# Where a norm's weight is multiplied in: into the weight units, or into the tokens' hi/lo parts (with the residual read from memory)

## The chip, the cores and the metric

The kernel runs on one core of a Trainium2 chip. The metric is the device time of one execution in microseconds, as the median over several runs. The core has five engines that run side by side, each with its own instruction queue: TensorE (PE, matmuls; PEld is its weight load), VectorE (DVE), ScalarE (ACT), GpSimd (POOL) and SyncE (SP), which in this kernel only issues DMAs. POOL issues some DMAs as well. An engine works its queue strictly in order, and a DMA-issuing instruction waits in its queue like any other. Instructions on different engines wait for each other by semaphores.

## The reference: what is computed

One inference step of a decoder trunk with two layers over T = 1032 tokens (1024 of a prompt, 8 decode tokens) and 1024 model dimensions, all in fp32. The parts that matter here:

```python
def rms_norm(x, w):
    y = x32 * lax.rsqrt(jnp.mean(x32 * x32, axis=-1, keepdims=True) + NORM_EPS)
    return (y * w.astype(jnp.float32)).astype(x.dtype)

for layer in range(DEPTH):                       # DEPTH = 2
    h = rms_norm(x, norm_mix[layer])
    if layer % 2 == 0:                           # layer 0: gated delta rule + retention
        out, ... = hybrid_mixer(h, ...)          # input projection, mixers, output projection w_out
    else:                                        # layer 1: state-space mixer
        out, ... = ssd_mixer(h, ...)
    x = x + out
    x = x + squared_relu_mlp(rms_norm(x, norm_mlp[layer]), mlp_w1[layer], mlp_w2[layer])
return rms_norm(x, norm_final), ...
```

Every sub-layer thus begins with a projection of `x * rstd * w`: `rstd` is one number for each token, `w` one number for each model dimension. The projection sums over the model dimension, so `w` can be multiplied into the rows of the weight matrix or into the rows of `x`, while `rstd` can be multiplied in after the sum.

## The kernel before

Tokens are kept transposed: 8 row tiles of 128 model dimensions by 1032 tokens. A product is made of three matmuls in a reduced format of fp32 (fp32r): each operand is split into a hi part and a lo part, and `mm3` (L147) adds whi·xhi (L150), whi·xlo (L151) and wlo·xhi (L152). The tokens' parts are the tiles `xh[k]` and `xl[k]`, which stay in SBUF for the length of a sub-layer; token columns go in three pieces of 344 (`NSL`).

**Weights.** `load_w` (L132) brings a unit of up to 512 columns from memory into `raw` (3 buffers, DMA from SP's queue, L136). If a norm weight is given, POOL multiplies the unit by it, in place (L140). ACT then rounds it to `whi` (L144), and DVE, or POOL for the units of the output and down projections, subtracts to get `wlo` (L145). `whi` and `wlo` share 6 buffers. The 264 units of the input projections (`wih`, `wis`) and of the MLP's up projections (`w` at `w1`) pass through L140; the units of the output projections (`woh`, `wos`) and of the down projections (`w2`) don't.

**Tokens.** At the start, `load_x` (L296) loads the 8 tiles of x (`xr`), and for each ACT rounds it to `xh` (L345) and DVE subtracts to `xl` (L346); POOL, ACT and DVE square and sum for the norm (L327, L328, L332). Later splits are made piece by piece by `split_piece` (L225), right after the last addition to a residual piece: ACT copies to `xh` (L229), DVE subtracts to `xl` (L230), ACT squares, POOL adds the square (L241). `rsqrt` (L243, its instruction is L250) is a POOL instruction everywhere, for the norms inside the mixers too (`rry`, `rs`, `nrs`).

**Stages in time.** Layer 0's mixer runs from 0 to about 735 us of the profiled execution, its last blocks of output projection to 800, its MLP to about 1520; layer 1's mixer runs to about 2320 and its MLP to the end. In a mixer, `proj` or `conv_tile`/`z` tiles are projected (72 units L140 fall between 1550 and 2250) while the recurrences of the chunks run in between: chains of small matmuls and DVE, ACT and POOL instructions. In layer 1's, POOL also multiplies the decode states (`dpr`, L1749, reduced by DVE at L1750) and issues the stores of states (L1747) and spilled outputs (L1505).

**Output projection.** Its weights are cut in blocks by input rows. The first block is done while the mixer's last work is running: `out_first` (L466) computes 8 row tiles m by 3 pieces n; DVE adds PSUM and `xh` into a stage tile `ost` (L473), POOL adds `xl` (L474), and SP stores it to `accd` in memory (L475). In layer 0 the pieces n = 0, 1 stage in a pair of buffers and n = 2 in a single one, so each is used once for each m; in layer 1 five buffers of two pools alternate. `out_proj` (L1328) then reloads the 8 sums (`acc<-accd`, L1335) and adds the later blocks into them (L1342); the last block's pieces are split at once by `split_piece`. `xh` and `xl` of the layer's input thus serve both as matmul operand and as the residual.

**MLP.** `up` projects a hidden tile, applies relu and the square (L1225 to L1228), and after each 4 tiles `down` (L1231) adds their part to `acc` (L1236). The last `down` of layer 0 splits its sums for layer 1; the last layer ends with `finish` (L1241), which takes the final norm in.

**Order.** The code is recorded once and scheduled by the framework, which puts each engine's instructions in the order of its own simulated times; the buffers' reuse makes the waits. The diff's places in the program therefore don't say where an instruction ends up in its queue.

Of the kernel before, what the change touches and what calls it, by code (L numbers as in the profile page):

```python
# [14 lines left out]
ALU = mybir.AluOpType  # L15
# [80 lines left out]
class Kern:  # L96
    def __init__(self, ctx, tc, I, O):
# [20 lines left out]
        self.xl = [self.xp.tile([P, T], F32R, name=f"xl{k}") for k in range(KT)]  # L118

# [12 lines left out]
    def load_w(self, src, n, normw=None, lo_eng=None, dst=None, norm_eng=None):  # L132
# [4 lines left out]
        if normw is not None:  # L137
            k = normw.shape[1]
            r3 = raw[:, :n].rearrange("p (k c) -> p k c", k=k)
            (norm_eng or nc.gpsimd).tensor_tensor(out=r3, in0=r3, in1=normw.unsqueeze(2).to_broadcast([P, k, n // k]), op=ALU.mult)  # L140
# [13 lines left out]
    def load_half(self, src, kh, M, normw):  # L154
        return self.load_w(src[:, kh * 4 * M:(kh + 1) * 4 * M], 4 * M, normw[:, kh * 4:kh * 4 + 4])
# [9 lines left out]
    def products(self, src, M, normw, pss):  # L165

        for kh in range(2):
            hi, lo = self.ahead.pop(0) if self.ahead else self.load_half(src, kh, M, normw)
# [12 lines left out]
    def gemm_units(self, src, M, normw, evict, other=False):  # L181
# [11 lines left out]
        for u, n in enumerate(self.products(src, M, normw, pss)):  # L193
# [13 lines left out]
    def gemm_flush(self, src, parts, evict):  # L207
# [3 lines left out]
        for m in range(8):  # L211
            w = []
            for k0 in range(0, kn, cut):
                k1 = min(kn, k0 + cut)
                hi, lo = self.load_w(src(m)[:, k0 * 128:k1 * 128], (k1 - k0) * 128, None, self.nc.gpsimd)
                w += [(hi[:, i:i + 128], lo[:, i:i + 128]) for i in range(0, (k1 - k0) * 128, 128)]
# [79 lines left out]
    def load_x(self, gp):  # L296
# [16 lines left out]
        w0 = [self.load_half(I["wih"][0], 0, 128, normw)]  # L313
# [30 lines left out]
        for m in range(KT):  # L344
            nc.scalar.copy(self.xh[m], xr[m])  # L345
            nc.vector.tensor_tensor(out=self.xl[m], in0=xr[m], in1=self.xh[m].bitcast(F32), op=ALU.subtract)  # L346
# [4 lines left out]
            if m == 1:  # L351
                w0.append(self.load_half(I["wih"][0], 1, 128, normw))
# [1552 lines left out]
```

## Time and profile before

| | |
|---|---|
| time, median of 3 runs | 3217.74 us (3217.33 to 3217.88) |
| profiled execution | 3203.04 us |
| its span (first to last instruction) | 3200.8 us |
| mean clock granted to TensorE | 0.973 |
| busy: PE / DVE / ACT / POOL | 3052.8 / 1724.0 / 841.2 / 1264.1 us |
| L140 on POOL | 264 instructions, 306.2 us |
| L474 on POOL | 48 instructions, median 928 ns |

The profiled execution is 14.7 us shorter than the median of the timed runs; 2.2 us of its time lie outside its span. A row of the profile names a line of the code, the engine, the operation, and the tiles by `out<-in`. In rows of a group, `x264 | 306.2, 1161 | 636.8 <-DMA raw<-w 330.0` means 264 instructions, 306.2 us busy, 1161 ns each, and 636.8 us in which the engine idled just before them, 330.0 of it until that DMA ended. In rows of the timeline the first number is the start in us, the second the duration, and brackets give the idle time just before it and what ended it. A row of a window gives, for each engine, its busy time in that stretch and, after PEclk, the granted clock.

### The profile page before, as it was taken

The numbers are of one execution on the slowest core, as the hardware profiler recorded it, in microseconds if no ns is written. First come the engines' busy times: TensorE is split into PE (matmuls) and PEld (weight loads), VectorE is DVE, ScalarE is ACT, GpSimd is POOL, SyncE is SP. The second block draws the span as 40 slices with busy tenths as digits, with TensorE's granted clock in tenths as the row PEclk, the third lists the DMA queues.
The fourth block names the chain that finished last, engine by engine and source line by source line (L and its number), as shares of the span: only waits on it lengthen the run. The fifth ranks groups of instructions, "written<-read, shape, count | busy, mean of one in ns | idle before, by whom it ended". The sixth has DMA issues, their size and how long they took to land. (4 is left out here: it accounts for less than half of the span.)

```text
span 3200.8 us, 49506 instructions
## 1 busy us (share of the span) xinstructions
PE 3052.8 (95%) x19758; PEld 2918.4 (91%) x19758; DVE 1724.0 (54%) x3189; ACT 841.2 (26%) x1604; POOL 1264.1 (39%) x1234
## 2 busy tenths in 40 slices
PE   7999999989999999999998999999899999999998
PEld 6888888879999999999987988897899999999998
DVE  7664767464333333335888696978635333333334
ACT  3221222214111111114344434343214111111112
POOL 4332324146323323335246556556625233232224
PEclk8899999889999999999999999999999999999999
DMA  3011103133111111111112121222531111111112
GB/s 122 23 44 59 47 22 105 42 132 116 47 47 47 47 48 48 48 47 46 42 52 65 50 84 58 80 74 96 186 109 44 50 47 47 47 47 47 47 49 71
DMA packets 102326, 202.14 MB, mean 63 GB/s; under 512 B 12624, under 2 KB 27728, under 8 KB 102096
## 3 DMA queue, kind: packets, MB, share of 16 engines
q1 hardware_dynamic: 94800, 173.82, 17.4%
q0 software_dynamic: 7296, 25.17, 2.0%
q8 instruction: 155, 2.54, 0.3%
q14 instruction: 75, 0.61, 0.1%
HBM read 157.94 MB, written 38.89 MB: 61 GB/s over the span
## 5 line engine op out<-in xcount | busy, mean ns | idle before, releaser
L150 PE MATMUL pg<-xh,whi 128*128 128x344 f32 x3072 | 1003.2, 327 | 10.8 <-DVE sxc L1460 4.8
L151 PE MATMUL pg<-xl,whi 128*128 128x344 f32 x3072 | 998.2, 325 | 0.0
L152 PE MATMUL pg<-xh,wlo 128*128 128x344 f32 x3072 | 997.2, 325 | 0.7 <-DVE wlo L145 0.7
L150 PEld LDWEIGHTS pg<-xh,whi 128*128 128x128 f32 x3072 | 585.5, 191 | 18.4 <-DVE sxc L1460 5.8
L144 ACT CAST whi<-raw 128x512 fp32r<-128x512 f32 (+2 forms) x443 | 271.6, 613 | 1257.9 <-PE pg L151 859.2
L152 PEld LDWEIGHTS pg<-xh,wlo 128*128 128x128 f32 x3072 | 585.2, 191 | 4.5 <-issue 1.7
L151 PEld LDWEIGHTS pg<-xl,whi 128*128 128x128 f32 x3072 | 584.2, 190 | 4.8 <-issue 2.8
L140 POOL TENSOR_TENSOR raw<-raw,vec 128x512 f32<-128x512 f32 x264 | 306.2, 1161 | 636.8 <-DMA raw<-w 330.0
L151 PE MATMUL pg<-alo,whi 128*128 128x344 f32 (+2 forms) x1476 | 472.4, 320 | 0.0
L152 PE MATMUL pg<-ahi,wlo 128*128 128x344 f32 (+2 forms) x1476 | 472.3, 320 | 0.0
L150 PE MATMUL pg<-ahi,whi 128*128 128x344 f32 (+2 forms) x1476 | 471.5, 319 | 0.0
L1236 DVE TENSOR_TENSOR acc<-acc,pg 128x344 f32<-128x344 f32 x360 | 183.1, 512 | 385.0 <-PE pg L152 384.7
L145 POOL TENSOR_TENSOR wlo<-raw,whi 128x512 fp32r<-128x512 f32 (+2 forms) x179 | 225.2, 1260 | 328.4 <-ACT whi L144 327.4
L145 DVE TENSOR_TENSOR wlo<-raw,whi 128x512 fp32r<-128x512 f32 x264 | 198.4, 752 | 195.6 <-ACT whi L144 185.8
L1227 POOL TENSOR_TENSOR r<-r 128x344 f32<-128x344 f32 x192 | 146.1, 762 | 386.0 <-ACT ahi L1226 337.3
L152 PEld LDWEIGHTS pg<-ahi,wlo 128*128 128x128 f32 x1476 | 277.6, 188 | 0.0
L150 PEld LDWEIGHTS pg<-ahi,whi 128*128 128x128 f32 x1476 | 277.5, 188 | 0.0
L151 PEld LDWEIGHTS pg<-alo,whi 128*128 128x128 f32 x1476 | 277.3, 188 | 0.0
L1228 DVE TENSOR_TENSOR alo<-r,ahi 128x344 fp32r<-128x344 f32 x192 | 135.5, 707 | 254.1 <-POOL r L1227 254.1
L1226 ACT ACTIVATE ahi<-r 128x344 fp32r<-128x344 f32 x192 | 94.7, 493 | 338.8 <-DVE r L1225 338.8
L1225 DVE SCALAR_TENSOR_TENSOR r<-pg,rstd_bc 128x344 f32<-128x344 f32 x186 | 94.9, 510 | 76.7 <-PE pg L152 75.4
L150 PE MATMUL pg<-mhi,whi 128*128 128x344 f32 x408 | 131.5, 323 | 4.9 <-DVE acc L1342 4.9
(540 smaller groups left out, 4439.8 us busy)
## 6 DMA issues: line engine op xcount, KB each, us to landing
raw<-w SPq DMA_DIRECT2D x256, 256.0 KB, 2.6
raw<-wis SPq DMA_DIRECT2D x80, 256.0 KB, 2.7
raw<-wih SPq DMA_DIRECT2D x56, 256.0 KB, 2.9
mraw<-spill SPq DMA_DIRECT2D x17, 512.0 KB, 4.1
accd<-ost SPq DMA_DIRECT2D x48, 172.0 KB, 2.5
acc<-accd SPq DMA_DIRECT2D x16, 516.0 KB, 6.9
dS<-sstate SPq DMA_DIRECT2D x32, 256.0 KB, 2.7
o_sssm<-dS POOLq DMA_DIRECT2D x32, 256.0 KB, 2.3
```

The costliest lines, as they stand in the source:

```text
L140: (norm_eng or nc.gpsimd).tensor_tensor(out=r3, in0=r3, in1=normw.unsqueeze(2).to_broadcast([P, k, n // k]), op=ALU.mult)
L144: nc.scalar.copy(hi[:, :n], raw[:, :n])
L145: (lo_eng or nc.vector).tensor_tensor(out=lo[:, :n], in0=raw[:, :n], in1=hi[:, :n].bitcast(F32), op=ALU.subtract)
L150: t.matmul(ps, lhsT=whi, rhs=xhi, start=start, stop=False)
L151: t.matmul(ps, lhsT=whi, rhs=xlo, start=False, stop=False)
L152: t.matmul(ps, lhsT=wlo, rhs=xhi, start=False, stop=stop)
L1225: nc.vector.scalar_tensor_tensor(out=r, in0=ps, scalar=0.0, in1=self.rstd_bc[:, s], op0=ALU.max, op1=ALU.mult)
L1226: nc.scalar.activation(hi[:, s], r, AF.Square)
L1227: nc.gpsimd.tensor_tensor(out=r, in0=r, in1=r, op=ALU.mult)
L1228: nc.vector.tensor_tensor(out=lo[:, s], in0=r, in1=hi[:, s].bitcast(F32), op=ALU.subtract)
L1236: nc.vector.tensor_tensor(out=s, in0=s, in1=ps, op=ALU.add)
```

## The change

The multiplication by the norm weight leaves `load_w` and goes into the split of the tokens: `xh` becomes the rounded `w*x`, and `xl` the rest of it, both with one scalar for each partition. ACT's copy becomes an activation with a scale (L229, L345), and DVE's subtraction an instruction that multiplies and subtracts (L230, L346). The 264 instructions at L140 and two small ones in the set-up of layer 1 (L1366) are gone.

`xh` and `xl` then no longer hold the residual. `out_first` now loads it from memory into the stage tile: in layer 0 from the kernel's input `xT`, in layer 1 from a new buffer `resd` in memory, which the last `down` of layer 0 fills, one DMA from POOL's queue for each m. DVE adds PSUM into the stage tile, and the addition on POOL (L474) is gone.

```diff
-    def load_w(self, src, n, normw=None, lo_eng=None, dst=None, norm_eng=None):
+    def load_w(self, src, n, lo_eng=None, dst=None):
...
         raw = self.wp.tile([P, 512], F32, tag="raw", name="raw", bufs=3)
         nc.sync.dma_start(raw[:, :n], src)
-        if normw is not None:
-            k = normw.shape[1]
-            r3 = raw[:, :n].rearrange("p (k c) -> p k c", k=k)
-            (norm_eng or nc.gpsimd).tensor_tensor(out=r3, in0=r3, in1=normw.unsqueeze(2).to_broadcast([P, k, n // k]), op=ALU.mult)
...
-    def split_piece(self, m, n, src, ssq, tp):
+    def split(self, m, s, src, w):
 
         nc = self.nc
-        s = NSL[n]
-        nc.scalar.copy(self.xh[m][:, s], src)
-        nc.vector.tensor_tensor(out=self.xl[m][:, s], in0=src, in1=self.xh[m][:, s].bitcast(F32), op=ALU.subtract)
+        nc.scalar.activation(self.xh[m][:, s], src, AF.Copy, scale=w)
+        nc.vector.scalar_tensor_tensor(out=self.xl[m][:, s], in0=src, scalar=w, in1=self.xh[m][:, s].bitcast(F32), op0=ALU.mult, op1=ALU.subtract)
+
+    def split_piece(self, m, n, src, ssq, tp, norm):
+
+        self.split(m, NSL[n], src, self.V(norm, m))
         self.square_piece(m, n, src, ssq, tp)
...
         for m in range(KT):
-            nc.scalar.copy(self.xh[m], xr[m])
-            nc.vector.tensor_tensor(out=self.xl[m], in0=xr[m], in1=self.xh[m].bitcast(F32), op=ALU.subtract)
+            self.split(m, slice(0, T), xr[m], self.V("mix0", m))
...
+            if l == 0:
+                self.resid = lambda m: self.I["xT"][:, m, :]
+            else:
+                self.resid = lambda m: self.resd[m]
...
             r = stage(n)
-            nc.vector.tensor_tensor(out=r, in0=ps, in1=self.xh[m][:, s].bitcast(F32), op=ALU.add)
-            nc.gpsimd.tensor_tensor(out=r, in0=r, in1=self.xl[m][:, s].bitcast(F32), op=ALU.add)
+            nc.sync.dma_start(r, self.resid(m)[:, s])
+            nc.vector.tensor_tensor(out=r, in0=r, in1=ps, op=ALU.add)
             nc.sync.dma_start(self.accd[m][:, s], r)
...
                     if b == HID // 4 - 1:
-                        self.split_piece(m, n, s, ssq, tp)
+                        self.split_piece(m, n, s, ssq, tp, "mix1")
+                        if n == 2:
+                            nc.gpsimd.dma_start(self.resd[m], acc[m])
...
-                nc.gpsimd.tensor_tensor(out=raw, in0=raw, in1=normw[:, k:k + 4].unsqueeze(2).to_broadcast([P, 4, 32]), op=ALU.mult)
```

What the schedule makes of it is seen in three places. The first is POOL's queue near the start of layer 1's chunks, at 1667 us of the profiled execution. Before:

```order
L1462 TENSOR_SCALAR sco<-sxc 128x11
L140 TENSOR_TENSOR raw<-raw,vec 128x512
L1749 TENSOR_TENSOR dpr<-dS,dbc 128x512 x2
L140 TENSOR_TENSOR raw<-raw,vec 128x512
L1457 MEMSET sxc 128x3
L1675 TENSOR_TENSOR x<-x,yi 128x4x128
L1682 TENSOR_TENSOR S<-S,segend 128x512
```

and with the change (lines are one lower there):

```order
L1461 TENSOR_SCALAR sco<-sxc 128x11
L1748 TENSOR_TENSOR dpr<-dS,dbc 128x512 x2
L1456 MEMSET sxc 128x3
L1674 TENSOR_TENSOR x<-x,yi 128x4x128
L1681 TENSOR_TENSOR S<-S,segend 128x512
```

The multiplications of weight units that stood ahead of and behind the two `dpr` are gone, and the rest keeps its order.

The second is SP's queue at the end of layer 0's `out_first`, at about 715 to 727 us, where the stores of the stage tiles, the loads of weight units and the reloads of the sums follow each other. Before:

```order
L475 DMA accd_6_103<-ost 128x344
L460 DMA mraw<-spill_7_96 128x1024
L136 DMA raw<-woh 128x384
L475 DMA accd_6_103<-ost 128x344
L475 DMA accd_7_104<-ost 128x344 x2
L136 DMA raw<-woh 128x256
L475 DMA accd_7_104<-ost 128x344
L1335 DMA acc_0_6973<-accd_0_97 128x1032
```

and with the change, where L477 is the load of the residual and L479 the store of the sum:

```order
L479 DMA accd_7_114<-ost 128x344
L477 DMA ost<-xT 128x344
L479 DMA accd_7_114<-ost 128x344
L138 DMA raw<-woh 128x256
L479 DMA accd_6_113<-ost 128x344
L477 DMA ost<-xT 128x344
L479 DMA accd_7_114<-ost 128x344
L138 DMA raw<-woh 128x384
L1338 DMA acc_0_6927<-accd_0_107 128x1032
```

The last piece of m = 7 now needs its load between the last store of m = 6 (the same stage buffer) and its own store, and all three stand ahead of the reloads of the sums in the one queue.

The third is POOL's queue at the border of the layers, about 1515 to 1540 us. Before:

```order
L241 TENSOR_TENSOR rstd_bc<-rstd_bc,sq 128x344 x2
L1393 MEMSET sx 128x288
L1457 MEMSET sxc 128x3 x2
L140 TENSOR_TENSOR raw<-raw,vec 128x512
L250 TENSOR_TENSOR rs<-ms,c_67 128x9
L140 TENSOR_TENSOR raw<-raw,vec 128x512 x2
L1462 TENSOR_SCALAR sco<-sxc 128x11
```

and with the change:

```order
L1241 DMA resd_95<-acc_6_6933 128x1032
L242 TENSOR_TENSOR rstd_bc<-rstd_bc,sq 128x344 x3
L1241 DMA resd_96<-acc_7_6934 128x1032
L242 TENSOR_TENSOR rstd_bc<-rstd_bc,sq 128x344
L1394 MEMSET sx 128x288
L251 TENSOR_TENSOR rs<-ms,c_67 128x9
L1456 MEMSET sxc 128x3 x2
L1461 TENSOR_SCALAR sco<-sxc 128x11
```

The stores of `resd` stand between the additions of squares, and the reciprocal root `rs` of the new norm has moved ahead of the two clears of `sxc`, with no weight unit in front of it.

More of the change, by code (lines that the diff above doesn't have):

```diff
@@ L118, in __init__ @@
         self.xl = [self.xp.tile([P, T], F32R, name=f"xl{k}") for k in range(KT)]
+        rp = ctx.enter_context(tc.tile_pool(name="resd", bufs=1, space=bass.MemoryType.DRAM))
+        self.resd = [rp.tile([P, T], F32, name=f"resd_{m}") for m in range(KT)]
     def V(self, name, i=0, n=1):
@@ L152, in mm3, with load_half @@
         t.matmul(ps, lhsT=wlo, rhs=xhi, start=False, stop=stop)
-    def load_half(self, src, kh, M, normw):
-        return self.load_w(src[:, kh * 4 * M:(kh + 1) * 4 * M], 4 * M, normw[:, kh * 4:kh * 4 + 4])
+    def load_half(self, src, kh, M):
+        return self.load_w(src[:, kh * 4 * M:(kh + 1) * 4 * M], 4 * M)
     def narrow(self, ps, w, x, k):
@@ L163, in narrow, with products @@
             self.nc.tensor.matmul(ps[32 * n:32 * n + M, 0:c.stop - c.start], lhsT=w, rhs=x[:, c], start=k == 0, stop=k == KT - 1)
-    def products(self, src, M, normw, pss):
+    def products(self, src, M, pss):
         for kh in range(2):
-            hi, lo = self.ahead.pop(0) if self.ahead else self.load_half(src, kh, M, normw)
+            hi, lo = self.ahead.pop(0) if self.ahead else self.load_half(src, kh, M)
             for n in range(3):
@@ L179, in others, with gemm_units @@
         return [self.pm(), self.ps2(), self.ps2()]
-    def gemm_units(self, src, M, normw, evict, other=False):
+    def gemm_units(self, src, M, evict, other=False):
         if self.first:
@@ L192, in gemm_units @@
         pss = self.others() if other else [self.pg() for n in range(3)]
-        for u, n in enumerate(self.products(src, M, normw, pss)):
+        for u, n in enumerate(self.products(src, M, pss)):
             if u == 0:
@@ L312, in load_x @@
         fetch(1)
-        w0 = [self.load_half(I["wih"][0], 0, 128, normw)]
+        w0 = [self.load_half(I["wih"][0], 0, 128)]
         nc.vector.tensor_scalar(out=self.ones_r, in0=self.ident, scalar1=0.0, scalar2=1.0, op0=ALU.mult, op1=ALU.add)
@@ L351, in load_x @@
             if m == 1:
-                w0.append(self.load_half(I["wih"][0], 1, 128, normw))
+                w0.append(self.load_half(I["wih"][0], 1, 128))
             if m > 1:
@@ L445, in layer @@
                 acc = [ap.tile([P, T], F32, name=f"acc{l}_{m}") for m in range(KT)]
-                self.out_proj(name, blocks, acc, tp, parts)
+                self.out_proj(name, blocks, acc, tp, parts, "mlp%d" % l)
             self.mlp(l, acc, l == 1)
@@ L486, in proj @@
         def proj(dst, off=0):
-            normw = self.V("mix0", 0, 8)
             def ev(n, ps):
                 nc.vector.tensor_tensor(out=dst[:, off + n * NW:off + (n + 1) * NW], in0=ps, in1=self.rstd_bc[:, NSL[n]], op=ALU.mult)
-            yield from self.gemm_units(I["wih"][next(wi)], 128, normw, ev)
+            yield from self.gemm_units(I["wih"][next(wi)], 128, ev)
         def gate(k, zs):
@@ L1228, in ev @@
                     nc.vector.tensor_tensor(out=lo[:, s], in0=r, in1=hi[:, s].bitcast(F32), op=ALU.subtract)
-                self.gemm_tile(I["w1"][l, t], 128, normw, ev, t == 1)
+                self.gemm_tile(I["w1"][l, t], 128, ev, t == 1)
             def down(b):
@@ L1325, in mlp, with out_proj @@
                 self.rstd = self.rstd_from()
-    def out_proj(self, name, blocks, acc, tp, parts):
+    def out_proj(self, name, blocks, acc, tp, parts, norm):
         nc, tc = self.nc, self.tc
@@ L1343, in ev @@
                     if last:
-                        self.split_piece(m, n, o, ssq, tp)
+                        self.split_piece(m, n, o, ssq, tp, norm)
                 for _ in self.gemm_flush(lambda m: self.I[name][m, :, c0 * 128:c0 * 128 + w], cur, ev):
@@ L1380, in ssm_setup @@
         self.first = self.others()
-        for u, _ in enumerate(self.products(I["wis"][4], 128, normw, self.first)):
+        for u, _ in enumerate(self.products(I["wis"][4], 128, self.first)):
             if u == 1:
@@ L1460, in ev @@
                 nc.vector.tensor_tensor(out=xc[:, 3 + n * NW:3 + (n + 1) * NW], in0=ps, in1=self.rstd_bc[:, NSL[n]], op=ALU.mult)
-            self.gemm_tile(I["wis"][ti // 4 * 10 + ti % 4 if ti < 16 else ti % 4 * 10 + ti // 4], 128, normw, ev)
+            self.gemm_tile(I["wis"][ti // 4 * 10 + ti % 4 if ti < 16 else ti % 4 * 10 + ti // 4], 128, ev)
             nc.gpsimd.tensor_scalar(out=gco, in0=xc[:, 3 + 1021:3 + 1032], scalar1=1.0, scalar2=None, op0=ALU.mult)
@@ L1485, in ev @@
                 nc.vector.scalar_tensor_tensor(out=z[:, NSL[n]], in0=ps, scalar=0.5, in1=self.rstd_bc[:, NSL[n]], op0=ALU.mult, op1=ALU.mult)
-            self.gemm_tile(I["wis"][g * 10 + 6 + i], 128, normw, ev)
+            self.gemm_tile(I["wis"][g * 10 + 6 + i], 128, ev)
             self.silu2(z, 1.0, gp)
```

7 lines of the change are left out of this document (2 added, 5 removed).

## The prediction

> **What bounds the kernel now.** First the page's head, then a table of windows cut at the stages (busy us and count for PE, PEld, DVE, ACT, POOL; then the granted clock, DMA share and GB/s).
>
> ```profile
> span 3200.8 us, 49506 instructions
> PE 3052.8 (95%) x19758; PEld 2918.4 (91%) x19758; DVE 1724.0 (54%) x3189; ACT 841.2 (26%) x1604; POOL 1264.1 (39%) x1234
> ...
> 0.00:40.00 40.00, 27.22 (x135) 17.02 (x135) 28.75 (x23) 17.08 (x21) 22.28 (x21) 0.87 0.58 187
> 40.00:640.00 600.00, 556.20 (x3838) 506.74 (x3836) 379.37 (x914) 150.06 (x316) 182.24 (x225) 0.92 0.16 49
> 640.00:735.00 95.00, 81.49 (x449) 69.93 (x449) 56.56 (x117) 20.17 (x36) 45.62 (x46) 0.87 0.45 153
> 735.00:800.00 65.00, 62.07 (x396) 61.01 (x395) 33.94 (x60) 27.30 (x62) 40.78 (x42) 1.00 0.24 82
> 800.00:1480.00 680.00, 680.00 (x4324) 680.00 (x4323) 238.97 (x427) 124.50 (x222) 209.87 (x214) 1.00 0.16 47
> 1480.00:1550.00 70.00, 67.43 (x436) 64.34 (x434) 50.48 (x93) 28.84 (x65) 39.46 (x41) 1.00 0.13 40
> 1550.00:2250.00 700.00, 652.03 (x4324) 598.40 (x4323) 559.95 (x884) 280.62 (x537) 385.61 (x320) 0.98 0.21 70
> 2250.00:2325.00 75.00, 64.99 (x397) 62.21 (x396) 42.01 (x72) 12.71 (x18) 44.13 (x41) 0.98 0.56 199
> ```
>
> TensorE sets the end: 148 us of the span (3200.8 - 3052.8) are all that any change outside it can win, short of a better clock. In the first MLP, 800 to 1480, PE idles 0.0 us, so nothing taken from POOL there is worth anything. The idle time lies in the mixers: 12.8 us at the start, 43.8 in 40 to 640, 13.5 in 640 to 735, 2.9 to 800, 2.6 at the layers' border, 48.0 in 1550 to 2250, 10.0 to 2325. There DVE is the busiest helper (559.95 of 700, 80%) and POOL is at 55%, so the question is how often POOL or DVE holds PE, and how often L140 or L474 is why.
>
> **What goes away, and where it lay.** The groups by line, the same windows for L140 alone, and the group of L474:
>
> ```profile
> L140 POOL TENSOR_TENSOR raw<-raw,vec 128x512 f32<-128x512 f32 x264 | 306.2, 1161 | 636.8 <-DMA raw<-w 330.0
> ...
> 40.00:640.00 600.00, 60.67 (x52) 0.92 0.16 49
> 1550.00:2250.00 700.00, 93.37 (x72) 0.98 0.21 70
> ...
> L474 POOL TENSOR_TENSOR ost<-ost,xl x48: 907/928/1916, 664.3 to 2310.4; 128x344 f32<-128x344 f32 x48
> ```
>
> Of 306.2 us only 154 lie in the two mixers, and they are not on PE's path as such: L140 acts by (a) standing in POOL's queue, often waiting for its DMA, ahead of an instruction that a chain needs, and (b) blocking DVE. I follow both through the timeline.
>
> **Layer 1's mixer, 1550 to 2250.** The clearest stall:
>
> ```profile
> 1704.39 1.04 POOL L140 TENSOR_TENSOR raw<-raw,vec 128x512 f32<-128x512 f32 x1 [0.49 <-DMA raw<-wis]
> 1705.39 2.62 POOL L1749 TENSOR_TENSOR dpr<-dS,dbc 128x512 f32<-128x512 f32 x2
> 1706.70 0.69 DVE L1750 TENSOR_REDUCE dy<-dpr 128x4 f32<-128x512 f32 x1 [2.31 <-POOL dpr L1749]
> ...
> 1709.38 0.48 PE L1665 MATMUL ps<-E,xdt 128*64 128x128 f32 x2 [2.85 <-DVE yi L1674]
> ...
> 1676.43 0.44 PE L1665 MATMUL ps<-E,xdt 128*64 128x128 f32 x4 [3.04 <-DVE yi L1674]
> 1805.59 0.33 PE L1665 MATMUL ps<-E,xdt 128*64 128x128 f32 x2 [1.15 <-DVE yi L1674]
> 2164.28 0.33 PE L1665 MATMUL ps<-E,xdt 128*64 128x128 f32 x2 [1.13 <-DVE yi L1674]
> 2051.14 1.19 PE L1677 MATMUL ps<-xd,sb 128*128 128x512 f32 x1 [2.19 <-DVE x L1667]
> ```
>
> L140 takes POOL at 1704.39 after 0.49 us of DMA wait; `dpr` starts 1.0 later for it, DVE waits 2.31 for `dpr`, and everything DVE has behind it, `yi` too, is late for PE. Without L140, `dpr` starts up to 1.5 us earlier (1.04 + 0.49), and DVE's wait shrinks by as much. Five stalls of PE have this chain (of the three small ones the first and the last stand above): 3.04 + 2.85 + 1.15 + 1.13 + 1.13 = 9.3 us; I take 6.4, since 1.5 of each of the first two come back and the three small ones can close (3.4). About a dozen more, of 0.5 to 2.2 us (the longest is the last row), follow a DVE instruction that was stretched while an L140 ran. They sum to about 15 us; I take a good third, 5.6, because DVE is 80% busy and its next instruction closes up only in part. Sum -12; from -5 (the five alone, halved) to -22 (nearly all of 24).
>
> On how DVE is stretched, the row at the kernel's start shows it plainly:
>
> ```profile
> 8.76 1.04 POOL L140 TENSOR_TENSOR raw<-raw,vec 128x512 f32<-128x512 f32 x1 [2.28 <-DMA raw<-wih]
> 8.85 2.04 DVE L346 TENSOR_TENSOR xl<-xr,xh 128x1032 fp32r<-128x1032 f32 x1 [0.78 <-ACT xh L345]
> ...
> 12.82 2.69 POOL L332 TENSOR_TENSOR sqx<-xr 128x1032 f32<-128x1032 f32 x1 [0.17 <-DMA xr<-xT]
> 13.67 2.39 DVE L145 TENSOR_TENSOR wlo<-raw,whi 128x512 fp32r<-128x512 f32 x1
> ...
> 16.11 0.46 PE L152 MATMUL pm<-xh,wlo 128*128 128x344 f32 x1 [3.16 <-DVE wlo L145]
> ```
>
> L145 takes 2.39 us beside POOL's L332 (12.82 to 15.51) against 0.68 alone, and L346 2.04 beside L140. [...]
>
> **The start, 0 to 40.** Without L140 at 8.76, L346 at 8.85 ends about 0.8 sooner (1.2 is its undisturbed time at 6.86), `whi` starts 1.08 earlier, and L145 falls before L332 rather than beside it. PE's 3.16 stall goes and some of what follows, while the first split must now wait for the norm weights: -5, from -8 to 0.
>
> **Layer 0's mixer, 40 to 800.** L140 stands ahead of `rry`, an rsqrt in the chain of the delta rule:
>
> ```profile
> 465.17 1.04 POOL L140 TENSOR_TENSOR raw<-raw,vec 128x512 f32<-128x512 f32 x1 [2.49 <-DMA raw<-wih]
> 466.16 1.04 POOL L250 TENSOR_TENSOR rry<-ssy,c 128x4 f32<-128x4 f32 x1
> 467.23 0.69 DVE L902 TENSOR_TENSOR Y<-Y,rry 128x512 f32<-128x512 f32 x1 [2.82 <-POOL rry L250]
> ...
> 467.98 0.33 PE L906 MATMUL ps<-c,Y 128*128 128x128 f32 x1 [2.50 <-DVE Y L902]
> ...
> 778.24 0.42 PE L152 MATMUL pg<-mhi,wlo 128*128 128x344 f32 x1 [1.81 <-POOL wlo L145]
> ```
>
> Two stalls of this kind (2.50 here, 1.43 at 169.93) and about 4 us of smaller ones after stretched DVE work: 40 to 640 gets -6, from -2 to -12 (a quarter of its 43.8). The 1.81 at 778.24 has an L140 1.5 us long ahead of the waited-for POOL work: -2, from -3 to 0.
>
> **Layer 0's `out_first`, the place that can lose.** Before, a stage buffer is used again once its store has landed; now it has to be stored, landed, loaded, landed and added into, and SP's one queue holds the load until the store has landed and everything behind it, the weight units of `woh` too.
>
> ```profile
> accd<-ost SPq DMA_DIRECT2D x48, 172.0 KB, 2.5
> raw<-woh SPq DMA_DIRECT2D x16, 192.0 KB, 2.5
> ...
> 710.37 0.52 DVE L473 TENSOR_TENSOR ost<-pg,xh 128x344 f32<-128x344 f32 x1 [2.37 <-DMA accd<-ost]
> 724.13 0.52 DVE L473 TENSOR_TENSOR ost<-pg,xh 128x344 f32<-128x344 f32 x1 [3.15 <-DMA accd<-ost]
> 724.73 1.84 POOL L474 TENSOR_TENSOR ost<-ost,xl 128x344 f32<-128x344 f32 x1 [0.84 <-DVE ost L473]
> ```
>
> The single buffer of n = 2 goes round once for each m. Before, from 710.37 to 724.13, three m took 13.8 us, 4.6 each. Now a round is a store's landing (2.5), a load's (2.5, by the row of 192 KB), DVE's 0.52 and two issues of about 0.3: 5.8 with one issue in the way, 6.1 with both; I take 5.8, hence +1.2 for each m after the buffers have filled, m4 to m7: +5. Against it, POOL's 48 additions of 0.93 us leave, and with them the last one ahead of the reload (1.84 us at 724.73): -1 to -2. I take +3, from -2 (loads hidden) to +9 (7 m, 8 us, and a late weight unit). This is no row of before; the 2.5 us is the nearest.
>
> **The layers' border, 1480 to 1550.** POOL loses 5 multiplications of 1.04 and gains 8 DMA issues, 0.58 each by `o_sssm<-dS` (L1747, 18.5 us for 32); `rs` no longer waits behind a unit. 0, from -2 to +3. Where acc is stored late, the clears of `sxc` wait for it, and behind them POOL's queue.
>
> **Layer 1's `out_first`.** Its end is a chain:
>
> ```profile
> 2310.36 1.92 POOL L474 TENSOR_TENSOR ost<-ost,xl 128x344 f32<-128x344 f32 x1
> 2312.30 0.32 SPq L475 DMA_DIRECT2D accd<-ost  x1
> ...
> 2317.34 0.62 PE L150 MATMUL pg<-mhi,whi 128*128 128x344 f32 x1 [3.18 <-DVE acc L1342]
> ```
>
> DVE's last addition starts at 2308.52 in the trace, so the store can go at about 2309.1, 3 us earlier, and the stall of 3.18 nearly closes. Five stage buffers leave the loads more room than layer 0's. -3, from -6 to +5 if the round trip shows here too.
>
> **What costs nothing.** The split: ACT's copy (482 ns for 344 columns at L229) becomes an activation like L1226 (493 ns); DVE's subtraction keeps its two SBUF inputs; the split follows the last addition while PE has other pieces. In the MLPs (800 to 1480, and after 2480) all is hidden behind full PE; should that cover go, it would be gains, not losses.
>
> **Sum.** -5 -6 +3 -2 +0 -12 -3 = -25 us: the profiled execution goes from 3203.0 to about 3178, and the median, 0.8% less as well, from 3217.7 to about **3193**.
>
> **Rivals.** (1) *The relief is hidden*: PE's stalls close only where L140 or its DMA wait stands in the chain itself (3 + 2.5 + 1.4 + 1.8 + 3 = about 12 us), the next releaser, mostly DVE at 80%, ends 4 later, and `out_first` returns 3: -5 us, 3213. For it: nearly all long waits of PE name DVE, not POOL. Against: DVE's own rows are stretched by POOL. (2) *Slower: the round trip through memory.* In both `out_first`s the stage's store-load-add takes 5.8 us against 4.6, SP's queue holds back `woh`/`wos` units and reloads: 8 x 1.2 = 10 in layer 0, 6 in layer 1, +3 at the border, with gains of 10: +9, 3227. It decides if PE, once a weight unit is late, loses over 1.5 us for each m. Against: layer 1 has five buffers, and 40 to 640 doesn't have this at all. (3) *The clock comes back too*: windows with idle PE have 0.92, 0.87 and 0.98 against 1.00 in the filled ones. Were half of 40 to 640's 0.08 regained (24 us of 600), it would be 3169 with the sum; the rows show the clock beside the gaps, not that it follows them. (4) *The schedule does not follow*: if the recorded order put the new loads ahead of weight units in 40 to 640, half the gain there would go; the order shows it at one place only, so it is in the range.
>
> **Chances.** The forecast 0.60 (3176 to 3208), rival 1 0.17, rival 2 0.10, rival 3 0.13. What a measurement can tell from no change is about 0.2%, 6.4 us: faster is below 3211.3. Of the forecast and rival 3 all is faster (0.73) and of rival 1 four tenths (0.07): 0.80; same 0.12; slower 0.08. The range, 3168 to 3213, leaves out rival 2, the upper half of rival 1 and the far end of rival 3.
>
> **What would show it.** After: POOL near 910 us busy (1264 less 306, less 50, plus 5); PE's wait for `yi` (L1674 before) gone from about 3 to 1.5 us at the two large places and closed at the small ones; `rry` right behind `ssy`; PE idle in 1550 to 2250 at about 36; the first matmul with `wlo` before 14 us; PE waiting in 640 to 735 for DVE, and DVE for the DMA `ost<-xT`, by 3 us more; 800 to 1480 full as before. It is wrong if DVE's wlo and xl rows don't get shorter, or if PE's idle in the mixers stays while POOL's busy time falls.

## The result, and the profile after

The changed kernel takes 3165.8 us, median of 4 runs (3164.0 to 3170.5), against 3217.5 us before (3203.7 to 3217.9): a ratio of 0.985, 95% interval 0.983 to 0.987. A second set of runs on another occasion gave 0.985 (0.982 to 0.989). It is faster by about 48 us in the mean of these runs, or 1.5% (the two medians lie 51.8 us apart); 25 us had been forecast for the median. One run of one experiment below, 3349.5 us at a granted clock of 0.833, was in a slower state of the chip and is left out of its median.

The page's head of the changed kernel:

```profile
span 3162.2 us, 48956 instructions
PE 3040.9 (96%) x19758; PEld 2914.6 (92%) x19758; DVE 1664.3 (53%) x3189; ACT 845.8 (27%) x1604; POOL 914.6 (29%) x928
```

POOL fell by 349.5 us and DVE by 59.7, although DVE has the same number of instructions (3189) and the new ones do more. PE's idle time went from 148.0 us (3200.8 - 3052.8) to 121.3, by 26.7. The rest of the 38.6 us by which the span shrank, 11.9 us, is busy time of PE, for the same 19758 matmuls. So the time that PE waits and the time that it works both shrank, and they have to be told apart in each stage.

The same DVE instruction can be found in both traces, so that the stages can be cut at equal work: the first `Y<-Y,rry` of the delta rule, the first `ost`, the first addition into `acc`, the first hidden tile of the MLP, the first `sxc` of layer 1, the last `yi` of its chunks, a hidden tile in the second MLP, the end. The windows before (length, then busy time and count of PE, PEld, DVE, ACT, POOL; then the granted clock, DMA share and GB/s):

```profile
0.00:169.20 169.20, 144.85 (x948) 125.61 (x948) 117.37 (x237) 54.58 (x100) 62.70 (x70) 0.90 0.22 70
169.20:663.70 494.50, 458.42 (x3109) 413.78 (x3109) 304.47 (x737) 117.85 (x247) 145.99 (x181) 0.91 0.18 56
663.70:731.20 67.50, 58.37 (x340) 51.03 (x340) 39.53 (x76) 12.45 (x19) 41.09 (x40) 0.94 0.46 152
731.20:797.60 66.40, 63.10 (x400) 62.04 (x400) 36.19 (x65) 28.26 (x65) 40.40 (x41) 1.00 0.29 104
797.60:1551.20 753.60, 750.86 (x4777) 747.77 (x4778) 291.71 (x524) 155.04 (x291) 250.09 (x254) 1.00 0.15 46
1551.20:2223.40 672.20, 628.79 (x4194) 576.45 (x4193) 533.84 (x851) 270.57 (x525) 369.69 (x309) 0.98 0.20 67
2223.40:2498.90 275.50, 259.69 (x1614) 254.72 (x1615) 149.20 (x248) 73.69 (x126) 129.17 (x113) 0.99 0.33 111
```

and with the change:

```profile
0.00:162.00 162.00, 141.50 (x948) 123.86 (x948) 111.44 (x237) 54.85 (x100) 38.22 (x51) 0.92 0.23 74
162.00:640.90 478.90, 449.90 (x3109) 406.49 (x3109) 295.59 (x737) 117.26 (x247) 104.63 (x144) 0.93 0.19 60
640.90:719.30 78.40, 60.88 (x340) 54.10 (x340) 36.11 (x75) 12.31 (x19) 15.27 (x16) 0.89 0.57 178
719.30:784.60 65.30, 64.35 (x400) 63.83 (x400) 34.62 (x65) 30.39 (x65) 31.78 (x33) 0.96 0.29 100
784.60:1535.90 751.30, 750.87 (x4780) 747.98 (x4779) 285.82 (x525) 156.95 (x291) 182.88 (x195) 1.00 0.17 52
1535.90:2187.00 651.10, 624.64 (x4194) 575.63 (x4194) 505.18 (x852) 269.81 (x525) 279.56 (x237) 0.98 0.21 69
2187.00:2459.70 272.70, 259.98 (x1614) 255.55 (x1615) 143.84 (x248) 75.88 (x126) 93.67 (x79) 0.98 0.38 127
```

Length less PE's busy time is PE's idle time. In a table, all in us, with the forecast's terms beside it:

| stage | forecast | measured | of it idle | of it PE busy |
|---|---|---|---|---|
| start, to the first `Y` | -5 (0 to 40) | -7.2 | -3.9 | -3.3 |
| layer 0's mixer, to the first `ost` | -6 (40 to 640) | -15.6 | -7.1 | -8.5 |
| layer 0's `out_first` | +3 | +10.9 | +8.4 | +2.5 |
| later output blocks, to the first hidden tile | -2 | -1.1 | -2.4 | +1.3 |
| first MLP, border, set-up of layer 1 | 0 | -2.3 | -2.3 | 0.0 |
| layer 1's mixer | -12 | -21.1 | -16.9 | -4.2 |
| its output projection | -3 | -2.8 | -3.1 | +0.3 |
| sum, with the second MLP's end | -25 | -38.6 | -26.7 | -11.9 |

The 60 us of L140 in the first MLP gave nothing: from its first to its last hidden tile the two traces keep one distance of 13.0 us.

**Where the idle time went.** In layer 1's mixer, the place that the prediction showed at 1704 us:

```profile
1684.50 0.69 POOL L1461 TENSOR_SCALAR sco<-sxc 128x11 f32<-128x11 f32 x1 [3.42 <-DVE sxc L1459]
1685.17 2.62 POOL L1748 TENSOR_TENSOR dpr<-dS,dbc 128x512 f32<-128x512 f32 x2
1686.46 0.69 DVE L1749 TENSOR_REDUCE dy<-dpr 128x4 f32<-128x512 f32 x1 [0.79 <-POOL dpr L1748]
1689.16 0.55 PE L1664 MATMUL ps<-E,xdt 128*64 128x128 f32 x6 [1.30 <-DVE yi L1673]
```

DVE waits 0.79 us for `dpr` instead of 2.31, and PE 1.30 instead of 2.85. In layer 0's mixer, at the `rry` shown at 465 us:

```profile
454.65 1.04 POOL L251 TENSOR_TENSOR rry<-ssy,c 128x4 f32<-128x4 f32 x1 [1.82 <-DVE ssy L901]
455.72 0.69 DVE L904 TENSOR_TENSOR Y<-Y,rry 128x512 f32<-128x512 f32 x1 [1.15 <-POOL rry L251]
456.47 0.66 PE L908 MATMUL ps<-c,Y 128*128 128x128 f32 x4 [0.82 <-DVE Y L904]
```

PE waits 0.82 instead of 2.50; POOL is free when `ssy` comes. In layer 0's first output block, the place that could lose, the change did lose:

```profile
682.22 0.42 SPq L477 DMA_DIRECT2D ost<-xT  x1
685.48 0.51 DVE L478 TENSOR_TENSOR ost<-ost,pg 128x344 f32<-128x344 f32 x1 [3.79 <-DMA ost<-xT]
686.05 0.43 PE L148 MATMUL pg<-of,whi 128*128 128x344 f32 x1 [4.39 <-DVE ost L478]
...
696.65 0.62 PE L148 MATMUL pg<-of,whi 128*128 128x344 f32 x1 [3.13 <-ACT mhi L466]
```

The residual's load is issued at 682.22 and lands 3.3 us later; DVE waits 3.79 for it and PE 4.39. Two more stalls, 2.85 and 5.52 us, follow at 710 and 720.

### The profile page after: what moved, and what is told of

It reads as the page before. It is cut to its first block, busy times and chain, and to the rows that moved or that the text cites. A ratio compares the mean times of both kernels' runs of the same rounds, so it can differ in the third digit from the quotient of the medians.

```text
span 3162.2 us, 48956 instructions
## 1 busy us (share of the span) xinstructions
PE 3040.9 (96%) x19758; PEld 2914.6 (92%) x19758; DVE 1664.3 (53%) x3189; ACT 845.8 (27%) x1604; POOL 914.6 (29%) x928
## 4 chain that ended last, share of the span: by engine, by line
PE 68%; DVE 6%; issue 1%; POOL 1%; ACT 1%; DMA 0%; SPq 0%; POOLq 0%; DVEq 0%; ACTq 0%
PE pg L148 21%; PE pg L150 21%; PE pg L149 21%; POOL dpr L1748 1%; DVE dS L1745 1%; DVE x L411 1%; PE ps L1664 1%; PE ps L1676 1%; DVE xl L227 0%; PE pm L1608 0%; PE pm L1610 0%; ACT xh L226 0%; PE ps L1670 0%; PE pm L1629 0%; PE pm L1613 0%
## 5 line engine op out<-in xcount | busy, mean ns | idle before, releaser
L143 DVE TENSOR_TENSOR wlo<-raw,whi 128x512 fp32r<-128x512 f32 x264 | 189.4, 718 | 191.2 <-ACT whi L142 183.2
L149 PE MATMUL pg<-mlo,whi 128*128 128x344 f32 x408 | 131.8, 323 | 0.0
```

The costliest lines, as they stand in the source:

```text
L143: (lo_eng or nc.vector).tensor_tensor(out=lo[:, :n], in0=raw[:, :n], in1=hi[:, :n].bitcast(F32), op=ALU.subtract)
L149: t.matmul(ps, lhsT=whi, rhs=xlo, start=False, stop=False)
```

## The experiments

The leading theory after the result had four claims: (A) the norm weights' half of the change wins some 45 us and the residual's half loses about 10 in layer 0; (B) L140 held PE through DVE, which a POOL instruction that reads SBUF was taken to block (in the kernel before, L346 took 2.04 us beside an L140 and 1.21 without), and through POOL's queue; (C) a stall of PE costs more than its length, since the granted clock falls behind it (in the kernel before it is 0.50 in the 5 us behind the stall of 3.20 that ended at 563.72); (D) the loss in layer 0 is the round trip of store and load through the one stage buffer of n = 2. The rivals stand with each.

**The residual alone.** The kernel before, with this and the stores of `resd`; the 264 multiplications stay:

```diff
-            nc.vector.tensor_tensor(out=r, in0=ps, in1=self.xh[m][:, s].bitcast(F32), op=ALU.add)
-            nc.gpsimd.tensor_tensor(out=r, in0=r, in1=self.xl[m][:, s].bitcast(F32), op=ALU.add)
+            nc.sync.dma_start(r, self.resid(m)[:, s])
+            nc.vector.tensor_tensor(out=r, in0=r, in1=ps, op=ALU.add)
```

> The kernel before with one half of the change: the output projection reads its residual from memory (loads into the stage tiles, stores of resd, no addition on POOL), while the norm weights stay on the weight units, with all 264 multiplications on POOL. Theory (the two halves are independent; this half costs 10 us in layer 0's first output block and wins 2 to 3 in layer 1's): profiled execution 3203 + 7 = about 3210. Rival (the loads are hidden when POOL is loaded anyway, and the loss in layer 0 comes only from the earlier arrival of the work): within 3 us of before, 3200 to 3206.

Measured: 3229.6 us, ratio to before 1.004 (1.002 to 1.006). This half alone makes the kernel slower, by 13 us in the medians where the theory gave 7. Layer 0's first output block takes 77.6 us with 60.4 busy, 17.2 idle, as in the changed kernel (17.5); its loss is the same with the 264 multiplications and without. The profile, 3229.2 us, was longer than the 3210 forecast: 10 us more than before's first profile have gathered by the first `Y` already, 9.5 of them PE's busy time at a clock of 0.85; see below on repeated runs.

**The norm weights alone.** The changed kernel with `out_first` as before (the two lines above the other way round) and without the stores of `resd`. The residual that it adds is the scaled one, not x: the same instructions, another sum.

> The changed kernel with the other half alone: norm weights scale the tokens' parts, no multiplication of weight units, but the residual is taken from xh and xl as before (DVE adds xh, POOL adds xl). The residual it adds is therefore the one scaled by the norm weight, not x itself: same instructions, another sum. Theory (independent halves): the profiled execution is 3203 - 46 = about 3157, 7 under the changed kernel; 640 to 735 loses nothing against before. Rival (half of the gain came from taking POOL's additions out of the two output blocks): 3165 or more.

Measured: 3158.6 us, ratio 0.982 (0.980 to 0.985), profile 3158.3. This half alone wins 1.8%, by its median more than both together (0.985), though the intervals touch. The two effects add up within the noise: 0.982 times 1.004 is 0.986, and both together measured 0.985. Layer 0's first output block takes 67.7 us, as before (67.5). Claim (A) stands, and the rival, 3165 or more, falls.

**Three multiplications put back.** In the kernel before, the longest stall of PE in layer 0's mixer was this, and the prediction had not counted it:

```profile
557.56 1.77 POOL L527 TENSOR_TENSOR xr<-xr,cs 128x344 f32<-128x344 f32 x2
558.49 4.42 DVE L528 TENSOR_TENSOR rf<-rf,xr 128x344 f32<-128x344 f32 x1 [0.22 <-POOL xr L527]
559.51 3.03 POOL L140 TENSOR_TENSOR raw<-raw,vec 128x512 f32<-128x512 f32 x3
563.39 0.68 DVE L811 TENSOR_TENSOR W<-pm,c 128x128 f32<-128x128 f32 x3
563.72 1.12 PE L807 MATMUL pm<-X,LT 128*128 128x64 f32 x4 [3.20 <-DVE W L811]
```

DVE's L528, 0.5 us alone and 1.2 here in the changed kernel, stands from 558.49 to 562.91, through three units of L140. `W`, behind it, is late for the triangular inverse. Into the changed kernel exactly these three were put back, by a tile of ones (`unit` counts the loads of input and up projections):

```diff
         nc.sync.dma_start(raw[:, :n], src)
+        if unit in (52, 53, 54):
+            r3 = raw[:, :n].rearrange("p (k c) -> p k c", k=4)
+            nc.gpsimd.tensor_tensor(out=r3, in0=r3, in1=self.ones[:, 0:4].unsqueeze(2).to_broadcast([P, 4, n // 4]), op=ALU.mult)
```

> The changed kernel with three multiplications put back on POOL, by a tile of ones, on the last-but-three to last-but-one weight units of layer 0's input projections, where the kernel before had three in a row at 559.5 us; all other instructions stand as in the changed kernel. Theory (a two-input instruction of DVE waits until the whole row of POOL's instructions is through, the chain of the triangular inverse is late, PE stalls about 3 us, and the granted clock falls for some 10 us behind the stall): DVE's rf<-rf,xr takes 4 us or more instead of 1.2 and the execution grows by 6 to 9 us, twice to three times the stall. Rival (the clock falls there anyway): it grows by the stall alone, 2.5 to 3.5 us. Second rival (the 3.2 us stall of before came from something else): no change.

Measured, in the trace of this kernel (L534 is the old L528, L813 the old L807):

```profile
548.33 4.42 DVE L534 TENSOR_TENSOR rf<-rf,xr 128x344 f32<-128x344 f32 x1 [0.22 <-POOL xr L533]
549.36 3.02 POOL L141 TENSOR_TENSOR raw<-raw,ones_r 128x512 f32<-128x512 f32 x3
553.56 1.11 PE L813 MATMUL pm<-X,LT 128*128 128x64 f32 x4 [3.20 <-DVE W L817]
```

and in windows of 5 us (length, PE's busy time, count of matmuls, granted clock):

```profile
545.00:550.00 5.00, 4.93 (x36) 1.00 0.41 137
550.00:555.00 5.00, 1.80 (x10) 0.79 0.64 215
555.00:560.00 5.00, 5.00 (x25) 0.53 0.00 0
560.00:565.00 5.00, 5.00 (x49) 1.00 0.41 123
```

The 4.42 and the 3.20 us are back to the hundredth. Behind the stall the clock is 0.79 and 0.53. In the changed kernel's trace the same work (540 to 560 us) ran at 1.00. The other profiles agree. In all four that have the three multiplications here (both of before, the residual alone, and this one) this instruction of DVE takes 4.42 us, PE stalls 3.2 and the clock falls to half before the stall is over. In the six without added work on POOL (both of the changed kernel, the norm weights alone, and the three variants of the residual further below) it takes 1.2, PE does not stall, and the clock stays full for 12 us and more. Across this place the distance between the two traces grows from 4.3 to 10.3 us, by 6.0: 3.2 of stall and 2.8 of slow clock. The whole kernel takes 3172.4 us, ratio 0.987 (0.985 to 0.990), about 7 above the first runs of the changed kernel, though not above its later ones (3173.0); the verdict rests on the trace at this place. The first theory holds; 6.0 is the lower end of what it gave. That the stall came from something else falls.

The stall of 3.20 us is not the shortest with a slow clock behind it: in the kernel before a stall of 2.14 us, which ended at 533.9 us, was followed by half speed from 535.2 on (0.76 in the window from 530 to 540). Length alone does not decide, though: behind a stall of 2.70 us that ended at 420.2 us in the same trace the clock stayed full for 16 us.

**Repeated profiles.** Both kernels again, unchanged, since before's first profile (3203 us) was shorter than its timed runs.

> The kernel before, unchanged, for a second profiled execution: its first one, 3203 us, lies 14 us under the median of its timed runs. Theory (the granted clock falls behind PE's stalls in some executions and not in others, with the same instructions): against the first profile the stages 800 to 1480 and 2480 to the end take the same time within 0.5 us, all difference lies in the two mixers, PE's idle time there is within 3 us of the first, and the rest is PE's busy time at a lower clock. Rival (something outside the core, memory or DMA, is slower in the longer executions): PE's idle time grows by the whole difference.

> The changed kernel, unchanged, on the chip and in the rounds of this call: ratio to before 0.983 to 0.987, a profile of 3160 to 3172 us. Theory (clock): its difference to the first profile of the changed kernel, if any, lies in the mixers and in the clock.

Measured: before 3212.1 us, ratio to itself 0.999 (0.997 to 1.001), profile span 3209.8; changed 3173.0, ratio 0.985 (0.982 to 0.989), span 3175.0. First and second stage of both second profiles, before first:

```profile
0.00:174.20 174.20, 150.24 (x948) 129.21 (x948) 117.78 (x237) 54.16 (x100) 61.56 (x70) 0.88 0.22 68
174.20:669.60 495.40, 458.96 (x3109) 414.76 (x3109) 305.13 (x737) 117.42 (x247) 145.39 (x181) 0.91 0.18 56
```

```profile
0.00:167.90 167.90, 147.99 (x948) 130.53 (x948) 111.95 (x236) 54.79 (x100) 37.88 (x51) 0.87 0.23 72
167.90:653.70 485.80, 455.89 (x3109) 412.66 (x3109) 295.95 (x736) 117.21 (x247) 104.61 (x145) 0.92 0.19 59
```

Between two executions of one program PE's idle time stays (24.0 against 24.4 in the first stage before; 19.9 against 20.5 after), and its busy time moves at another clock (150.2 against 144.9; 148.0 against 141.5). Over the whole span, idle is 148.0 and 146.1 before, 121.3 and 123.1 after; busy is 3052.8 and 3063.7 before, 3040.9 and 3051.9 after. So the change took about 25 us of stalls (26.7 and 23.0 in the two pairs) and 12 us of PE's busy time (11.9 and 11.8), at a slower clock before; but that busy time varies by 11 us between two executions of one kernel. The same instructions with the same gaps can meet the slow clock or not. A gap of 1.53 us at 409 us stands alike in the first profile of the changed kernel and in that with three units back (which differs from it only later); the window behind it, first in the one, then in the other:

```profile
410.00:415.00 5.00, 4.75 (x40) 1.00 0.18 54
```

```profile
410.00:415.00 5.00, 5.00 (x25) 0.50 0.18 54
```

40 matmuls in the one, 25 in the other, and more than 5 us of distance between the traces by 419 us. In the first the clock stays full for 14 us behind the gap, to 423.6 us; in the second it is at half within about 1 us (0.95 in the window from 405 to 410) and for 13.7 us in all. What decides is open. The clock records of the first traces of before and of the changed kernel hold the values 1 and 0.5 alone; the stretches at 0.5 in them (23 and 22, without the last of each, in which the trace ends) last 3.41, 6.83, 10.24, 13.65 or 17.07 us.

The two pairs of profiles lie 38.6 and 34.8 us apart, so 9 to 13 us of the timed 48 are in neither. The record has the span and the mean granted clock of every timed run beside the second profiles: the 13 of before go from 3204.2 us at 0.973 to 3221.2 at 0.967, about 2.5 us for each 0.001. Their mean clock is 0.969, and before's first profile had 0.973, worth some 10 us. The rest thus goes with the clock too, as far as the record shows.

**POOL's time, with and without reading SBUF.** Two kernels with POOL work ahead of each of the 264 weight loads of the changed kernel: two clears, or one product of constants, both overwritten by the load.

```diff
+        if unit is not None:
+            nc.gpsimd.memset(raw[:, :n], 0.0)
+            nc.gpsimd.memset(raw[:, :n], 0.0)
         nc.sync.dma_start(raw[:, :n], src)
```

```diff
+        if unit is not None:
+            v = self.c0[:, 0:4].unsqueeze(2).to_broadcast([P, 4, n // 4])
+            nc.gpsimd.tensor_tensor(out=raw[:, :n].rearrange("p (k c) -> p k c", k=4), in0=v, in1=v, op=ALU.mult)
         nc.sync.dma_start(raw[:, :n], src)
```

> The changed kernel in which POOL clears the raw buffer twice ahead of each of the 264 weight loads of the input and up projections (two memsets of 128x512, about 1.2 us by the rate of the 128x288 one, 0.34 us): POOL's time is taken as by the multiplications, but nothing is read, and it stands ahead of the DMA instead of behind it. Theory (most of the gain came from DVE, which a POOL instruction that reads SBUF had blocked): DVE's busy time stays within 10 us of the changed kernel's 1664, and the execution grows by less than 10 us, to 3165 to 3174. Rival (POOL's queue was the matter: what stands behind the extra instructions is late): it grows by 20 us or more.

> The same place in the changed kernel, with one POOL product of two constant tiles into the raw buffer (128x512, reads SBUF, about 1.04 us) instead of the two clears; the DMA overwrites it. Theory (blocking of DVE): DVE's busy time grows by 25 to 50 us, and the execution by 15 to 35 us more than with the clears. Rival (POOL's queue): no more than with the clears, which are longer.

Measured: clears 3192.2 us, ratio 0.994 (0.991 to 0.996); products 3227.7 us, ratio 1.004 (1.001 to 1.006). For the clears the head of the page and POOL's groups, then both for the products:

```profile
PE 3057.5 (96%) x19758; PEld 2927.3 (92%) x19758; DVE 1667.5 (52%) x3189; ACT 846.7 (27%) x1604; POOL 1185.1 (37%) x1456
```

```profile
L140 POOL MEMSET raw<- 128x512 f32 x264 | 138.6, 525 | 13.2
L139 POOL MEMSET raw<- 128x512 f32 x264 | 138.5, 525 | 441.0 <-DVE wlo L146 413.2 <-issue 10.0 <-PE pg L165 7.0
```

```profile
PE 3077.9 (95%) x19758; PEld 2944.7 (91%) x19758; DVE 1741.3 (54%) x3189; ACT 846.5 (26%) x1604; POOL 1195.0 (37%) x1192
```

```profile
L140 POOL TENSOR_TENSOR raw<-c 128x512 f32<-128x512 f32 x264 | 287.0, 1088 | 455.8 <-DVE wlo L146 404.5 <-issue 31.2 <-ACT V L717 5.3
```

POOL is taken for nearly as long (277 and 287 us). The clears leave DVE where it was (1667.5 against 1664.3), the products add 77 us to it (25 to 50 were forecast), and 35 us more to the time. So the blocking of DVE is real here, and of these two kinds of POOL work only the products, which read SBUF, did it. But the clears cost 19 to 26 us against the changed kernel's 3173.0 and 3165.8, where the theory gave less than 10 and the rival 20 or more: POOL's queue counts as well. Both ways of claim (B) stand, but not the theory that most of the gain came through DVE. PE's idle time in the two mixers (from the first `Y` to the first `ost`, and layer 1's) says how they share: 29.0 + 26.5 = 55.5 us changed, 35.2 + 32.0 = 67.2 with clears, 40.9 + 40.6 = 81.5 with products, 36.1 + 43.4 = 79.5 before. Of the 24 us between changed and before, about half (11.7) goes with the time on POOL; the other half is left for the blocking of DVE. The extra work stands ahead of the loads here, where L140 stood behind them, so the shares are rough (the products reach 81.5, past before's 79.5); L140's wait for its DMA at the head of the queue wasn't tried by itself.

**The residual's loads from ScalarE's queue.**

```diff
-            nc.sync.dma_start(r, self.resid(m)[:, s])
+            nc.scalar.dma_start(r, self.resid(m)[:, s])
```

> The changed kernel with the residual loads issued from ScalarE's queue rather than SyncE's. Theory (the loss in layer 0 is SyncE's one queue: a load stands behind mraw loads and stores that wait): the loss of 10 us there shrinks to under 5, the profiled execution is 3155 to 3160. Rival (the loss is the round trip of store and load through the single stage buffer of n = 2): 3162 to 3166. Second rival: the wait for the stage buffer in ScalarE's queue holds back the rounding of weight units, slower than the changed kernel by up to 10.

Measured: 3175.0 us, ratio 0.987 (0.983 to 0.991): no gain over the changed kernel's 3165.8 and 3173.0. Layer 0's first output block takes 74.2 us with 57.8 busy, 16.4 idle; the idle time is hardly less than the changed kernel's 17.5. SyncE's queue, as the place where the loads wait, is not the main cause. Whether the second rival adds the few us on top is not shown.

**More stage buffers.** For every second m the three pieces stage in one of three tiles that are free there:

```diff
         def stage(n):
+            if n == 0:
+                stage.i += 1
+            if stage.i % 2:
+                if n == 0:
+                    stage.t = gp.tile([P, T], F32, tag="z", name="ost", bufs=3)
+                return stage.t[:, NSL[n]]
```

> The changed kernel with more room for the stage tiles of layer 0's first output block: for every second m the three pieces stage in one of three tiles of 1032 columns that the mixer no longer uses there, so that the single buffer of n = 2 goes round once for two m. Theory (the loss of 11 us there is the round trip of store and load through the single buffer): PE's wait of 4.4 us for the addition goes and the loss shrinks to 2 to 4 us, the execution to 3153 to 3158. Rival (SyncE's queue, where loads stand behind waiting stores): 3160 to 3166.

Measured: 3156.6 us, ratio 0.982 (0.981 to 0.984). Layer 0's first output block in windows (PE alone: length, busy, clock), with the residual from ScalarE's queue above and more stage buffers below:

```profile
651.40:725.60 74.20, 57.81 (x340) 0.94 0.58 184
```

```profile
645.50:711.00 65.50, 57.41 (x321) 0.90 0.62 202
```

8.1 us idle instead of 17.5, and 9.1 before the change (19 matmuls of the block stand ahead of this cut here). From the first `rv` of the retention to the first addition into `acc`, a cut that is alike in all, it is 447.5 us against the changed kernel's 455.6. The longest stall in the block is 2.0 us instead of 5.5. So the loss is the round trip through too few stage buffers. That it is mainly the single buffer of n = 2, as claim (D) has it, is seen in the changed kernel's trace by the order of DVE's 24 additions: the two long waits for a load, 3.79 and 6.14 us, are those of n = 2 in m = 4 and m = 7, while the pair's longest are 1.31 and 1.24. The profiles of the residual alone and of the changed kernel's second run show the same. In the run here none of the 24 additions waits for a load.

**Layer 0's residual from the parts.** DVE takes the norm weight out again, `winv` being its reciprocal, so that layer 0 loads nothing; layer 1 reads from memory.

```diff
+            if name == "woh":
...
+                v = self.winv[:, m:m + 1]
+                nc.vector.scalar_tensor_tensor(out=r, in0=self.xh[m][:, s].bitcast(F32), scalar=v, in1=ps, op0=ALU.mult, op1=ALU.add)
+                nc.vector.scalar_tensor_tensor(out=r, in0=self.xl[m][:, s].bitcast(F32), scalar=v, in1=r, op0=ALU.mult, op1=ALU.add)
+            else:
+                nc.sync.dma_start(r, self.resid(m)[:, s])
+                nc.vector.tensor_tensor(out=r, in0=r, in1=ps, op=ALU.add)
```

> The changed kernel with layer 0's residual taken from xh and xl again: DVE multiplies both by the reciprocal of the norm weight and adds them to PSUM, two DVE instructions of about 0.5 us for each piece, no loads and nothing on POOL; layer 1 reads its residual from memory as in the changed kernel. Theory (the two layers' halves are independent): layer 0's loss of 11 us goes, layer 1 keeps its gain, the execution takes 3151 to 3155, faster than all so far. Rival (the second DVE instruction with two SBUF inputs is blocked by POOL's wlo there and takes the place of the loads): 3158 to 3166.

Measured: 3153.0 us (3149.8 to 3155.1), ratio 0.981 (0.979 to 0.983), the lowest median of all, as the theory had it. That output block takes 65.8 us with 56.9 busy. The second DVE instruction is blocked little:

```profile
L483 DVE SCALAR_TENSOR_TENSOR ost<-xl,winv,ost 128x344 f32<-128x344 f32 x24 | 14.4, 617 | 0.0
L482 DVE SCALAR_TENSOR_TENSOR ost<-xh,winv,pg 128x344 f32<-128x344 f32 x24 | 13.0, 564 | 5.2 <-PE pg L150 5.2
```

Two instructions of 617 and 564 ns take the place of one of 510: 15 us more of DVE's time in 24 pieces, for a loss of 11 us removed. It needs norm weights that are not zero.

## Why the prediction came out as it did

The direction, the bound (stalls of PE in the mixers, nothing in the MLPs) and the sum of the stalls were right: -25 forecast, -26.7 and -23.0 in the two pairs of profiles. That the sum agrees so closely is in part luck: layer 1's mixer gave 5 us more than its term, layer 0's `out_first` lost 5 more than its own, and the two errors cancel. And the whole time fell about twice as far as forecast: the median, 3165.8, lies 2 us below the range of 3168 to 3213, and the sum, which holds stalls alone, had no term for PE's busy time, which fell too. Step by step:

- *Layer 1's mixer, -12.* Measured -16.9 of stalls. The two large `yi` stalls closed by 1.94 and 1.55, as forecast (1.5 each). The three small ones, which the step let close entirely, did not move (1.15, 1.13, 1.13 became 1.17, 1.16, 1.17): there L140 had not held `dpr` back. In the changed kernel's trace POOL idles 6.25 us and more ahead of `dpr` at these places, and `dpr` starts no earlier beside DVE's work. The dozen smaller stalls behind stretched DVE instructions, of which the step took "a good third", gave most of the gain; the 1.90 and 1.88 us for `sxc` went entirely, while the 2.19 for `x` stayed. "DVE is 80% busy and its next instruction closes up only in part" was the wrong reason. DVE's busy time in this stage fell from 533.8 to 505.2 us; that its backlog went with it is the likely reason for the larger gain, argued and not tested.
- *Layer 0's mixer, -6.* Measured -7.1 and -6.5 of stalls, and 8.5 and 3.1 of busy time beside them. The `rry` stalls shrank from 2.50 to 0.82 and from 1.43 to 0.83, where the step had counted on most of both. But the step listed the wrong places: the 3.20 at 563.72 was a chain of three L140, DVE's L528, `W` and PE, and I had followed PE's wait to `W` and no further back to why DVE was late. Put back alone, it costs 6.0 us.
- *The start, -5.* The first matmul with `wlo` starts at 11.79 instead of 16.11; -7.2 and -6.3 by the first `Y` in the two pairs, of it -3.9 and -4.1 idle.
- *Layer 0's `out_first`, +3.* The mechanism was right, the size wrong: +10.9, of which 8.4 idle; the idle time lies at the end of the step's range (+9), the whole beyond it. It priced 1.2 us for each of four m, in a steady round through one buffer with landings of 2.5 us. Its 4.6 us for a round of before was a misreading: by the order of the 24 additions the row at 710.37 is a piece n = 0 (of m = 5), which uses the pair, and the one at 724.13 is n = 2 of m = 7. The n = 2 of m = 4 to 7 start at 706.31, 713.72, 719.62 and 724.13, 5.9 us apart in the mean; with the change at 685.48, 691.17, 699.60 and 709.70, 8.1 apart. The loads took 3.1 us (median of the 24 `ost<-xT`) and the stores 2.9; loads of `mraw` and stores that wait stood between them in the queue (which weighs little: with the loads off that queue 16.4 of the 17.5 us of idle time stayed); and a late sum delayed the reload of `acc` too (5.52 us where it had been 1.67). The bound "+9" used the landing time of a calmer queue.
- *The border, 0; the later blocks, -2; layer 1's `out_first`, -3.* -2.3, -1.1 and -2.8. (The recorded "L140 1.5 us long" ahead of 778.24 is its wait for a DMA, 1.52; it ran 1.04.) The last store of layer 1's sums goes 0.5 us after the start of DVE's addition instead of 3.8, and the 3.18 stall for `acc` shrank to 1.81. Five stage buffers left the loads enough room.
- *The clock*, which stood as a rival of its own with 0.13. It turned out not to be a rival but to come with the stalls: in both pairs PE's busy time fell by 12 us beside them, though not every stall meets the slow clock (the one of 2.70 us at 420.2 did not). The rows "0.92 beside 1.00" were said to "show the clock beside the gaps, not that it follows them"; with three units put back it follows (0.79 and 0.53). Adding these 12 us would have put the median near 3181.
- *The rival "slower: the round trip through memory"* was the effect of one half of the change, in layer 0 alone; by itself this half makes the kernel slower by 0.4%.
- POOL's busy time, forecast near 910, is 914.6.

## What to carry to other kernels

Follow a stall of the bounding engine back past its releaser, to why the releaser was late: here a helper's instruction at more than eight times its usual length (4.42 us for 0.51) had another engine's row of instructions beside it. A stall can cost more than its length, since the granted clock may fall behind it: 2.8 us behind a stall of 3.2 at the place tested, and 12 us beside 25 us of stalls over this kernel. An operand that was at hand in SBUF is not free to replace by a load where its buffer goes round through a store: count one landing each way, under the load of that stage (here 2.9 us for the stores and 3.1 for the loads, by their medians), and give it a second buffer or rebuild it from what is there.

## What was not expected of the hardware

A DVE instruction with two SBUF inputs that fell on a row of POOL instructions was not let in between them here: 4.42 us for 0.5 us of work, through the end of two `xr` products, a short one and three of 1.01 us. Beside POOL's clears DVE's busy time stayed (1667.5 us against 1664.3), beside its products it grew by 77 us. The granted clock differed between executions of one program (0.973 and 0.970 before, 0.976 and 0.971 with the change) by enough to move PE's busy time by 11 us, at the same idle time within 2.
